# Merging two matmuls that share a stationary operand: u's high and low parts as one 512-column moving operand, with a PSUM pool of 6 + 2 banks

## The chip, the cores and the metric

The kernel runs on one core of one Trainium2 chip. The metric is the device time of one execution in microseconds (us). Three executions before the change took 1532.24, 1532.51 and 1533.59 us; their median, 1532.51 us, is the time that the prediction is made against. TensorE is called PE here, VectorE DVE, ScalarE ACT, GpSimd POOL; SP issues most DMAs.

## What is computed

One decoder layer on 256 tokens of width 2048, all in float32:

```python
u   = rmsnorm(h, norm_mix_pre)
z, xbc, dt_raw, q, k, v = split(u @ w_in)           # 2048 x 12320
y_ssm = SSD scan on silu(conv(xbc)), gate silu(z), grouped RMSNorm
y_att = dilated causal attention on q, k, v (16 heads of 128)
h   = h + rmsnorm(concat(y_ssm, y_att) @ w_out, norm_mix_post)
h   = h + rmsnorm(relu(rmsnorm(h) @ w_up)**2 @ w_down, norm_mlp_post)
```

The four weight matrices hold most of the work: w_in, w_out (4096 x 2048), w_up (2048 x 8192) and w_down (8192 x 2048). All are read once from HBM.

## The kernel before, in words

**Every product in three.** To keep float32 accuracy with PE's faster fp32r format, each operand is cut into a high part (rounded to fp32r) and a low part (what the rounding left). A product a·b becomes hi·hi + hi·lo + lo·hi, three matmuls into the same accumulator. `split` (line 117) makes the parts: ACT copies to the high part (line 120, or 123 with a scale), DVE subtracts it (line 121 or 124).

**Weights.** `weights` (line 126) loads a block of KB = 2 row tiles by 512 columns (512 KB) by a DMA on SP's queue into `raw` (4 buffers), and splits it into `hi` and `lo` (5 buffers each). All of it is issued under `tc.high_priority(offset=AHEAD)`. The order of instructions on each engine is not the order of the Python lines: a planner at build time places each engine's instructions by priority as soon as, by its own durations, their inputs and buffers are there. The finished order on each engine is fixed, and an instruction that waits holds up all behind it on its engine.

**Two kinds of product.** `gemm_tokens` (line 157) gives [token, feature] results: the activations are stationary, the weights move, 512 columns a matmul, three matmuls (lines 174, 175, 176) for each token half and row tile. It takes two accumulators of one PSUM bank each. It serves z, v, w_out, the first block of w_up and w_down. `gemm_features` (line 182) gives [feature, token] results: a 128x128 piece of the weights is stationary, and u moves, 256 tokens a matmul. For each row tile k (16) and each of four feature tiles f it issues line 197 (`hi`·`uh`), line 199 (`hi`·`ul`) and line 200 (`lo`·`uh`), into `acc[f // 2][:, f % 2]`, half a bank. It takes two accumulators of one bank each. There are 31 such calls: 8 for the convolved blocks (B, C, x), 8 for q and k, 15 for w_up. So each of the three lines runs 31 x 64 = 1984 times.

**PSUM.** Eight banks: pool `pacc` with 4 accumulators of one bank and pool `psm` with 4 of one bank, the latter handed out by `psmall` (line 108) to everything else: turned tiles of x (`turn_x`, 251), the SSD groups (`ssd_group`, 393), attention (486), `residual` (567).

**What reads the accumulators of gemm_features.** `conv_block` (368): DVE multiplies the accumulator by 1/rms into `pad` (line 375), then 16 DVE and 4 ACT instructions convolve. `queries` (515): DVE multiplies it into `cT` (line 519). The w_up loop (657): one DVE instruction does relu times 1/rms into `r` (line 660), then `hidden` squares it on ACT (616) and splits it. Each call has two such reads, b = 0 and 1, of 512 columns.

**Side work.** The SSD groups and attention heads are Python generators in the deque `waiting`; `pump` (146) runs one step after each weight block, so that their small matmuls stand between the blocks. Two SSD groups are under way at a time. A group's first step takes two `ps` buffers (lines 399, 410), its second one (433) that the third step still writes and reads (438 on PE, 440 on DVE), and the third step takes another (443) for the 16 matmuls of line 446.

**The start.** The first `gemm_features` call loads x as it goes: `turn_x` transposes a piece of x on PE (line 256) into a `ps` buffer and splits it into `uh` and `ul`. With `step=1` the weight block is loaded and split one row tile at a time.

## Time and profile before

| | |
|---|---|
| three executions | 1532.24, 1532.51, 1533.59 us |
| the profiled execution: its own time | 1533.54 us |
| its span, first to last instruction | 1531.8 us |
| matmuls recorded | 9701 |
| granted PE clock, mean | 0.999 |
| DVE busy, ACT busy, shares of the span | 57%, 47% |
| DMA: moved, mean rate | 283.38 MB, 185 GB/s |

How to read the views. The page lists each engine's busy time; a matmul's busy time includes its way through the array, and the next starts while it is still on that way, so the sum of busy times is more than the time PE needed. What one matmul costs in a dense row is the distance from its start to the start of the next, which the timeline shows. In the timeline the columns are start, duration, engine, line, operation, tiles (out<-in), shape and count. A row of a group gives count, busy time, mean duration in ns, and the idle time before it. A row of the waits gives who waited for whom: total us, times, longest.

### The profile page before, as it was taken

The numbers are of one execution on the slowest core, as the hardware profiler recorded it, in microseconds if no ns is written. First come the engines' busy times: TensorE is split into PE (matmuls) and PEld (weight loads), VectorE is DVE, ScalarE is ACT, GpSimd is POOL, SyncE is SP. The second block draws the span as 40 slices with busy tenths as digits, with TensorE's granted clock in tenths as the row PEclk, the third lists the DMA queues.
The fourth block names the chain that finished last, engine by engine and source line by source line (L and its number), as shares of the span: only waits on it lengthen the run. The fifth ranks groups of instructions, "written<-read, shape, count | busy, mean of one in ns | idle before, by whom it ended". The sixth has DMA issues, their size and how long they took to land.

```text
span 1531.8 us, 23944 instructions
## 1 busy us (share of the span) xinstructions
PE 1516.7 (99%) x9701; PEld 1384.2 (90%) x9701; DVE 874.8 (57%) x1196; ACT 713.3 (47%) x945; POOL 57.7 (4%) x73
## 2 busy tenths in 40 slices
PE   8999999999999999999999999999999999999997
PEld 8999999999999999888878999988889999988886
DVE  5777786875555454544457545544444555554444
ACT  6555564554535343544346444444444444444432
POOL 0002200220000000000000000000000000000000
PEclk9999999999999999999999999999999999999999
DMA  8565556555655555575556556555566666555553
GB/s 266 175 197 170 185 178 188 177 167 165 177 167 169 173 169 171 173 259 195 190 180 205 181 180 184 186 193 193 192 192 193 180 182 187 182 191 193 193 171 132
DMA packets 147951, 283.38 MB, mean 185 GB/s; under 512 B 11408, under 2 KB 14336, under 8 KB 147328
## 3 DMA queue, kind: packets, MB, share of 16 engines
q1 hardware_dynamic: 142576, 271.94, 57.1%
q10 hardware_dynamic: 5264, 9.91, 1.9%
q8 instruction: 76, 1.25, 0.3%
q14 instruction: 35, 0.29, 0.0%
HBM read 279.68 MB, written 2.13 MB: 184 GB/s over the span
## 4 chain that ended last, share of the span: by engine, by line
PE 98%; DMA 1%; DVE 1%; issue 0%; ACT 0%; POOL 0%; SPq 0%; POOLq 0%; DVEq 0%
PE acc L197 16%; PE acc L199 16%; PE acc L200 16%; PE acc L174 15%; PE acc L176 15%; PE acc L175 15%; PE ps L446 1%; PE ps L511 0%; PE ps L489 0%; DMA xs<-in_x_dram 0%; DMA raw<-in_w_in_dram 0%; PE ps L402 0%; PE ps L488 0%; PE ps L512 0%; PE ps L466 0%
## 5 line engine op out<-in xcount | busy, mean ns | idle before, releaser
L121 DVE TENSOR_TENSOR lo<-raw,hi 128x1024 fp32r<-128x1024 f32 (+1 forms) x520 | 629.4, 1212 | 575.6 <-ACT hi L120 574.3
L120 ACT ACTIVATE hi<-raw 128x1024 fp32r<-128x1024 f32 (+1 forms) x520 | 543.3, 1046 | 733.4 <-PE acc L176 332.7
L197 PE MATMUL acc<-uh,hi 128*128 128x256 f32 x1984 | 569.6, 288 | 1.8 <-ACT uh L123 1.8
L199 PE MATMUL acc<-ul,hi 128*128 128x256 f32 x1984 | 562.4, 284 | 0.0
L200 PE MATMUL acc<-uh,lo 128*128 128x256 f32 x1984 | 562.0, 283 | 0.0
L197 PEld LDWEIGHTS acc<-uh,hi 128*128 128x128 f32 x1984 | 380.9, 192 | 3.5 <-ACT uh L123 2.4
L199 PEld LDWEIGHTS acc<-ul,hi 128*128 128x128 f32 x1984 | 381.6, 192 | 1.3 <-DVE ul L124 0.4
L200 PEld LDWEIGHTS acc<-uh,lo 128*128 128x128 f32 x1984 | 381.4, 192 | 0.0
L174 PE MATMUL acc<-hi,sh 128*128 128x512 f32 x384 | 150.6, 392 | 0.0
L174 PE MATMUL acc<-hi,ah 128*128 128x512 f32 x384 | 149.9, 390 | 0.0
L175 PE MATMUL acc<-lo,sh 128*128 128x512 f32 x384 | 149.5, 389 | 0.0
L176 PE MATMUL acc<-hi,sl 128*128 128x512 f32 x384 | 149.4, 389 | 0.0
L176 PE MATMUL acc<-hi,al 128*128 128x512 f32 x384 | 149.4, 389 | 0.0
L175 PE MATMUL acc<-lo,ah 128*128 128x512 f32 x384 | 149.4, 389 | 0.0
L174 PE MATMUL acc<-hi,uh 128*128 128x512 f32 x288 | 112.5, 392 | 0.0
L176 PE MATMUL acc<-hi,ul 128*128 128x512 f32 x288 | 112.1, 391 | 0.0
L175 PE MATMUL acc<-lo,uh 128*128 128x512 f32 x288 | 112.0, 390 | 0.0
L176 PEld LDWEIGHTS acc<-hi,sl 128*128 128x128 f32 x384 | 72.1, 188 | 15.1
L176 PEld LDWEIGHTS acc<-hi,al 128*128 128x128 f32 x384 | 72.1, 188 | 15.0
L175 PEld LDWEIGHTS acc<-lo,ah 128*128 128x128 f32 x384 | 72.1, 188 | 14.9
L175 PEld LDWEIGHTS acc<-lo,sh 128*128 128x128 f32 x384 | 72.1, 188 | 14.8
L174 PEld LDWEIGHTS acc<-hi,sh 128*128 128x128 f32 x384 | 72.1, 188 | 14.8
(181 smaller groups left out, 962.2 us busy)
## 6 DMA issues: line engine op xcount, KB each, us to landing
raw<-in_w_in_dram SPq DMA_DIRECT2D x184, 512.0 KB, 3.6
raw<-in_w_up_dram SPq DMA_DIRECT2D x128, 512.0 KB, 3.6
raw<-in_w_down_dram SPq DMA_DIRECT2D x128, 512.0 KB, 3.6
raw<-in_w_out_dram SPq DMA_DIRECT2D x64, 512.0 KB, 4.1
raw<-in_w_in_dram SPq DMA_DIRECT2D x16, 256.0 KB, 5.2
bc<-acs_d ACTq DMA_DIRECT2D x8, 512.0 KB, 4.4
xs<-in_x_dram SPq DMA_DIRECT2D x8, 256.0 KB, 5.3
h<-in_x_dram ACTq DMA_DIRECT2D x1, 2048.0 KB, 12.0
```

The source lines that it names most:

```text
L120: nc.scalar.activation(hi, src, AF.Copy)
L121: nc.vector.tensor_tensor(lo, src, hi.bitcast(F32), op=ALU.subtract)
L174: nc.tensor.matmul(acc[t], a_h[:, r, ts], hi[:, j], start=k == 0, stop=False)
L175: nc.tensor.matmul(acc[t], a_h[:, r, ts], lo[:, j], start=False, stop=False)
L176: nc.tensor.matmul(acc[t], a_l[:, r, ts], hi[:, j], start=False, stop=k == nk - 1)
L197: nc.tensor.matmul(dst, hi[:, j, fs], uh[:, k], start=k == 0 and f % 2 == 0, stop=False, skip_group_check=True)
L199: nc.tensor.matmul(dst, hi[:, j, fs], ul[:, k], start=False, stop=False, skip_group_check=True)
L200: nc.tensor.matmul(dst, lo[:, j, fs], uh[:, k], start=False, stop=last, skip_group_check=True)
L446: nc.tensor.matmul(p[:, c, r], bc[:, r, c * P:(c + 1) * P], xdt[:, c, r], start=True, stop=True)
```

## The change

Five edits:

1. `uh` and `ul` become the two halves of one tile `u2` [128, 16, 2, 256], so that for one row tile the two parts lie side by side: 512 columns.
2. `gemm_features` multiplies `hi` by all 512 columns in one matmul, into a full bank whose first half collects hi·uh and whose second half collects hi·ul. The matmul `lo`·`uh` goes to the first half. Each accumulator is now a tile of two banks, two of them a call. The loops change places: feature tiles outside, the block's two row tiles inside.
3. `added` puts the halves together: ACT copies the second halves (512 columns) out of PSUM, DVE adds the first halves. It stands under `tc.high_priority(offset=AHEAD)`. The three readers then work on its result in SBUF: one ACT and one DVE instruction more for each of the 62 reads.
4. `pacc` has 3 tiles of two banks (6 banks), `psm` 2 of one bank. `gemm_tokens` takes one two-bank tile, a bank for each token half.
5. At the start one of the two-bank tiles, `spare`, stands in for the lost `ps` buffers: `turn_x` uses `psmall` and the banks of `spare` by turns.

```diff
-    pacc = ctx.enter_context(tc.tile_pool(name="pacc", bufs=4, space=bass.MemoryType.PSUM))
-    psm = ctx.enter_context(tc.tile_pool(name="psm", bufs=4, space=bass.MemoryType.PSUM))
+    pacc = ctx.enter_context(tc.tile_pool(name="pacc", bufs=3, space=bass.MemoryType.PSUM))
+    psm = ctx.enter_context(tc.tile_pool(name="psm", bufs=2, space=bass.MemoryType.PSUM))
...
-    uh = big.tile([P, NK, S], F32R, name="uh")
-    ul = big.tile([P, NK, S], F32R, name="ul")
+    u2 = big.tile([P, NK, 2, S], F32R, name="u2")
+    uh, ul = u2[:, :, 0], u2[:, :, 1]
...
-        acc = [pacc.tile([P, NB], F32, name="acc") for _ in range(NT)]
+        both = pacc.tile([P, NT, NB], F32, name="acc")
+        acc = [both[:, t] for t in range(NT)]
...
-        acc = [pacc.tile([P, 2, S], F32, name="acc") for _ in range(2)]
+        acc = [pacc.tile([P, 2, 2, S], F32, name="acc") for _ in range(2)]
...
-            for j in range(KB):
-                k = k0 + j
-                for f in range(4):
-                    dst = acc[f // 2][:, f % 2]
-                    fs = slice(f * P, (f + 1) * P)
-                    last = k == NK - 1
-                    nc.tensor.matmul(dst, hi[:, j, fs], uh[:, k], start=k == 0 and f % 2 == 0, stop=False,
+            for f in range(4):
+                fs = slice(f * P, (f + 1) * P)
+                bank = acc[f // 2][:, f % 2]
+                for j in range(KB):
+                    k = k0 + j
+                    nc.tensor.matmul(bank, hi[:, j, fs], u2[:, k], start=k == 0, stop=False, skip_group_check=True)
+                    nc.tensor.matmul(bank[:, 0], lo[:, j, fs], uh[:, k], start=False, stop=k == NK - 1,
                                      skip_group_check=True)
-                    nc.tensor.matmul(dst, hi[:, j, fs], ul[:, k], start=False, stop=False, skip_group_check=True)
-                    nc.tensor.matmul(dst, lo[:, j, fs], uh[:, k], start=False, stop=last, skip_group_check=True)
...
+    def added(dst, acc, tmp=None):
+
+        tmp = dst if tmp is None else tmp
+        with tc.high_priority(offset=AHEAD):
+            nc.scalar.activation(tmp, acc[:, :, 1], AF.Copy)
+            nc.vector.tensor_tensor(dst, acc[:, :, 0], tmp, op=ALU.add)
...
+    spare = pacc.tile([P, 2, NB], F32, name="acc")
+
     def turn_x(k0):
-        q = psmall().rearrange("p (f s) -> p f s", f=2)
+        i = k0 // KB
+        q = (spare[:, i // 2 % 2] if i % 2 else psmall()).rearrange("p (f s) -> p f s", f=2)
...
-            nc.vector.tensor_tensor(pad[:, :, 3:], acc[b], rbc[:, None, :].to_broadcast([P, 2, S]), op=ALU.mult)
+            added(pad[:, :, 3:], acc[b], dst[:, 2 * b:2 * b + 2])
+            nc.vector.tensor_tensor(pad[:, :, 3:], pad[:, :, 3:], rbc[:, None, :].to_broadcast([P, 2, S]), op=ALU.mult)
...
-            nc.vector.tensor_tensor(dst[:, 2 * b:2 * b + 2], acc[b], scale[:, None, :].to_broadcast([P, 2, S]),
-                                    op=ALU.mult)
+            d = dst[:, 2 * b:2 * b + 2]
+            added(d, acc[b])
+            nc.vector.tensor_tensor(d, d, scale[:, None, :].to_broadcast([P, 2, S]), op=ALU.mult)
...
-                nc.vector.scalar_tensor_tensor(r, acc[b], 0.0, rbc[:, None, :].to_broadcast([P, 2, S]),
+                added(r, acc[b])
+                nc.vector.scalar_tensor_tensor(r, r, 0.0, rbc[:, None, :].to_broadcast([P, 2, S]),
                                                op0=ALU.max, op1=ALU.mult)
```

## The prediction

> **What bounds the kernel now.** I read the page first: busy times, then the chain of work that ended last.
>
> ```profile
> span 1531.8 us, 23944 instructions
> ...
> PE 1516.7 (99%) x9701; PEld 1384.2 (90%) x9701; DVE 874.8 (57%) x1196; ACT 713.3 (47%) x945; POOL 57.7 (4%) x73
> ...
> PE 98%; DMA 1%; DVE 1%; issue 0%; ACT 0%; POOL 0%; SPq 0%; POOLq 0%; DVEq 0%
> PE acc L197 16%; PE acc L199 16%; PE acc L200 16%; PE acc L174 15%; PE acc L176 15%; PE acc L175 15%; PE ps L446 1%; PE ps L511 0%; PE ps L489 0%; DMA xs<-in_x_dram 0%; DMA raw<-in_w_in_dram 0%; PE ps L402 0%; PE ps L488 0%; PE ps L512 0%; PE ps L466 0%
> ```
>
> 98% of the chain is PE's, and half of that is the three lines of `gemm_features`. A busy PE could still hide waits, so the next view is PE's own waits between 40 and 1517 us:
>
> ```profile
> PE ps L580 <- PE acc L176: 0.5, 1, 0.5
> PE ps L580 <- DVE h L575: 0.4, 1, 0.4
> ```
>
> Two waits, 0.9 us in all. PE is dense, so the time is the number of matmuls times their distance from start to start. That distance comes from PE's timeline at the edges of two stretches of the MLP:
>
> ```profile
> 990.32 0.40 PE L174 MATMUL acc<-hi,sh 128*128 128x512 f32 x1
> ...
> 1164.20 0.39 PE L176 MATMUL acc<-hi,al 128*128 128x512 f32 x1
> 1164.42 0.28 PE L197 MATMUL acc<-uh,hi 128*128 128x256 f32 x1
> ...
> 1348.62 0.28 PE L200 MATMUL acc<-uh,lo 128*128 128x256 f32 x1
> 1348.74 0.40 PE L174 MATMUL acc<-hi,sh 128*128 128x512 f32 x1
> ```
>
> From 990.32 to 1164.42 lie four `gemm_tokens` calls of 32 row tiles: 4 x 32 x 2 x 3 = 768 matmuls of 512 columns in 174.10 us, **226.7 ns each**. From 1164.42 to 1348.74 lie eight `gemm_features` calls: 8 x 64 x 3 = 1536 matmuls of 256 columns in 184.32 us, **120.0 ns each**. Two of 256 cost 240.0, one of 512 costs 226.7: 13.3 ns go with the instruction and not with its columns.
>
> **The merge.** The line that goes and the one that grows run 1984 times each:
>
> ```profile
> L197 PE MATMUL acc<-uh,hi 128*128 128x256 f32 x1984 | 569.6, 288 | 1.8 <-ACT uh L123 1.8
> L199 PE MATMUL acc<-ul,hi 128*128 128x256 f32 x1984 | 562.4, 284 | 0.0
> ```
>
> Per step the three matmuls took 360.0 ns; after, one of 512 and one of 256 take 226.7 + 120.0 = 346.7. Saved: 13.3 ns x 1984 = **26.4 us**. This needs the two widths to alternate at the price that each has in a row of its own kind. The edge above shows one pair of each: 0.22 us from the 512-column matmul at 1164.20 to the 256-column one behind it, 0.12 us from the 256 at 1348.62 to the 512 behind it. The other worry is the loading of weights, of which one per step goes too: if a load were longer than the matmul that hides it, the 256-column one would be the bound. The floor for it shows at 16 matmuls of 64 columns:
>
> ```profile
> 132.76 1.73 PE ps L446 x16
> ```
>
> 1.73 / 16 = 108 ns, under 120: a load hides behind a 256-column matmul, as it does now. I take 26.4 us.
>
> The Trainium skill speaks against this size: "TensorE: Matmul & The Clock Gate", section "Back-to-back issue gap", has a warm matmul cost N/2.4 + 2.5 ns. By it 256 columns cost 109.2 and 512 cost 215.8, the merge saves 2.5 ns a step, an estimate of 5 us in all. Both distances measured here are above that rule, and their difference, the only thing that counts, is 13.3.
>
> **What is added, on ACT and DVE.** Each of the 62 reads gets an ACT copy and a DVE add of 512 columns out of PSUM. Nothing in the trace reads every second 256 columns; the nearest rows read a whole bank, and I take them:
>
> ```profile
> L670 ACT ACTIVATE mw<-acc 128x512 f32<-128x512 f32 x8 | 4.7, 589 | 1.2 <-PE acc L176 1.2
> L660 DVE SCALAR_TENSOR_TENSOR r<-acc,rbc 128x512 f32<-128x512 f32 x30 | 20.8, 692 | 0.4
> ```
>
> 62 x 0.589 = 36.5 us on ACT, 62 x 0.69 = 42.8 us on DVE, spread over the kernel, beside PE: cost nothing as long as nobody waits. DVE's load by stretch, from the windows (length, then busy PE, PEld, DVE, ACT, POOL, clock, DMA share, GB/s):
>
> ```profile
> 118.00:165.00 47.00, 47.00 (x318) 43.35 (x317) 39.56 (x78) 26.52 (x39) 10.82 (x12) 1.00 0.54 169
> 990.32:1164.42 174.10, 174.10 (x770) 144.15 (x769) 80.61 (x68) 73.73 (x75) 0.00 (x0) 1.00 0.60 193
> 1164.43:1348.73 184.30, 184.30 (x1537) 184.30 (x1536) 97.40 (x93) 82.04 (x93) 0.00 (x0) 1.00 0.62 184
> ```
>
> In the w_up stretch DVE goes from 53% to (97.4 + 16 x 0.69) / 177.5 = 61%. The tightest is the SSD stretch: 39.56 of 47 us, and with one call's two adds 41 of 46: 89%. Neither engine becomes the bound. Nor does the memory: the weights of the w_up stretch, 184 GB/s now, come to 184 x 184.3 / 177.5 = 191 GB/s, which the token stretch (193) shows to be had.
>
> **Where PE may have to wait: the hand-over of accumulators.** Three two-bank tiles in turn and two for each `gemm_features` call mean that where two such calls follow each other, the second tile of the later one is the first tile of the earlier. Counting the turns through the kernel gives 21 such hand-overs: 4 at the convolved blocks, 4 at k after q, 13 in w_up. The changed loop order works for it: the first tile (feature tiles 0 and 1) is done half a block before the call's end T, and wanted half a block after. A block is 8 steps x 347 ns = 2.77 us, so the tile is done at T - 1.39 and wanted at T + 1.39. In between must go the copy and the add. What else the two engines do then, around the call's end at 1187.46 in the stretch before:
>
> ```profile
> 1184.66 1.06 ACT L120 ACTIVATE hi<-raw 128x1024 fp32r<-128x1024 f32 x1 [1.82 <-PE acc L199]
> 1185.75 1.23 DVE L121 TENSOR_TENSOR lo<-raw,hi 128x1024 fp32r<-128x1024 f32 x1 [1.65 <-ACT hi L120]
> 1186.94 1.41 DVE L660 SCALAR_TENSOR_TENSOR r<-acc,rbc 128x512 f32<-128x512 f32 x2
> ```
>
> Each block's end releases a weight split: ACT 0.08 us after the end, then DVE at 1.2, done at 2.4. So with the shorter block ACT is free at T - 1.6, the copy runs from T - 1.3 to T - 0.7; DVE's split ends at T - 0.4, the add ends near T + 0.3. Wanted at T + 1.39: 1.1 us to spare. Behind the waiting copy on ACT stands the next weight split, behind the add the same on DVE; five weight buffers, some 11 us ahead, cover that. I take 0 for the hand-overs.
>
> **psm with two buffers.** In attention the steps come 3.5 us apart, and each takes one buffer:
>
> ```profile
> 399.21 0.43 PE ps L489 x2
> 402.74 0.43 PE ps L489 x2
> ```
>
> ```profile
> L489 PE MATMUL ps<-cT x32: 379/380/382, 399.0 to 632.2; 128*128 128x256 f32 x32
> L495 DVE CUSTOM_DVE_ANT_0 sm<-ps,cst x32: 291/355/423, 399.7 to 635.9; 128x128 f32<-128x128 f32 x16, 128x256 f32<-128x256 f32 x16
> ```
>
> With two, a buffer is wanted again after 7 us; the last one, written by 632.6, was read by 636.3, 3.7 us: 0. The SSD groups are tighter. With four buffers, the tile of line 446 was free at once; with two it is the tile that line 438 has just written, and must wait until DVE's line 440 has read it:
>
> ```profile
> 132.16 0.60 PE L438 MATMUL ps<-st,cT 128*128 128x256 f32 x2
> 132.59 0.55 PE L446 MATMUL ps<-xdt,bc 128*128 128x64 f32 x4
> ...
> 137.25 0.60 PE L438 MATMUL ps<-st,cT 128*128 128x256 f32 x2
> 137.68 0.44 PE L446 MATMUL ps<-xdt,bc 128*128 128x64 f32 x3
> ```
>
> ```profile
> 132.79 0.42 DVE L440 TENSOR_TENSOR yo<-ps,eacs 128x256 f32<-128x256 f32 x1 [1.54 <-PE ps L438]
> ...
> 139.10 0.42 DVE L440 TENSOR_TENSOR yo<-ps,eacs 128x256 f32<-128x256 f32 x1
> ```
>
> If PE stood still, it would lose 133.21 - 132.59 = 0.6 us for one group of a pair and 139.52 - 137.68 = 1.8 for the other, 4 x 2.4 = 9.8 us for eight groups. The planner may instead put matmuls of the running call in between, and then it is 0. I take **2 us**, nearer to 0, because such matmuls are always there. With them the moved groups cost PE nothing.
>
> **The start.** Here PE waits for x, and the memory is the bound (first row, 0.95 and 311 GB/s); its matmuls of 256 columns stand 0.21 us apart up to 15.5 us and 0.12 from then on:
>
> ```profile
> 5.00:15.00 10.00, 7.49 (x32) 6.79 (x33) 4.69 (x9) 5.61 (x13) 0.00 (x0) 1.00 0.95 311
> ```
>
> ```profile
> 15.04 0.41 PE L199 MATMUL acc<-ul,hi 128*128 128x256 f32 x1
> 15.25 0.41 PE L200 MATMUL acc<-uh,lo 128*128 128x256 f32 x1
> ...
> 15.94 0.28 PE L197 MATMUL acc<-uh,hi 128*128 128x256 f32 x1
> 16.06 0.28 PE L199 MATMUL acc<-ul,hi 128*128 128x256 f32 x1
> ...
> 32.03 1.04 PE L256 MATMUL ps<-cst,xs 128*128 128x128 f32 x8
> ```
>
> ```profile
> PE acc L197 <- ACT uh L123: 1.8, 2, 1.2
> PE ps L256 <- DMA xs<-in_x_dram: 2.4, 2, 1.3
> ```
>
> With the feature tiles outside, PE wants both row tiles of a block early, so the waits that there are (4.2 us) may come to twice that: +4. If the slow distance ends 20 matmuls sooner, that is 20 x 0.09 = 2 us: -2. I take **+1 us**. The second call, whose first tile is now `spare`, loses nothing that counts: the last pieces of x are transposed at 32.03, so the first call was still running then.
>
> **Sum.** -26.4 + 0 + 2 + 1 = -23.4 us. The profiled execution took 1533.54 us (span 1531.8 and 1.7 around it), 1.0 over the median of the three; against the median: 1532.5 - 23.4 = **1509 us**.
>
> **Rivals.**
>
> *A. As above*, 1503 to 1514: the merge, with 0 to 10 us of waits. Chance 0.62.
>
> *B. The merge pays, the waits take a good part.* The SSD stretch is where DVE is at 89%, and there both the hand-overs (4) and the two `ps` buffers (every step of eight groups) wait for DVE in its order. For it speaks that a read of `ps` already comes up to 2 us after PE's write (139.10 against 137.25); against it that PE waits nowhere now. Price: 9.8 us of the bound above and some half a us at each of 16 further steps: 1532.5 - 26.4 + 18 = 1524 at its end, 1514 at its near end. Chance 0.20.
>
> *C. The merge does not pay.* If a 512-column matmul over the two halves costs what two do, or only little less, the time is 1532.5 less a few: 1527 to 1535. Against it stand the 768 matmuls at 226.7. Chance 0.06: 0.02 for a gain of 5 us, 1527.5, and 0.04 for none. The figure of 2.5 ns in the Trainium skill's "TensorE: Matmul & The Clock Gate", "Back-to-back issue gap", would be the former.
>
> *D. Slower: the hand-over.* The place is the add of `added` on DVE at the 21 hand-overs. If the planner puts copy and add behind the weight split that the call's last block releases, ACT splits until T + 1.14, DVE until T + 2.37, and the add ends at T + 3.06, 1.67 us after PE wants the tile: 21 x 1.67 = 35 us, and 1532.5 - 26.4 + 35 = **1541 us**. It decides from 26.4 / 21 = 1.26 us a hand-over on. For it: the order is fixed at build time by the planner's durations, and splits and adds have the same offset. Against it: the add belongs to the earlier call and its input is there half a block sooner. Chance 0.12.
>
> **How the numbers follow.** A measurement of this kernel can tell about 0.2%, 3 us, from no change. Faster by more: A, B and the 0.02 of C, 0.84; within: the 0.04; slower: D, 0.12. The range takes all of A and nearly all of B: 1503 to 1525, about 0.8.
>
> **What the changed profile would show.** PE with 9701 - 1984 = 7717 matmuls; the w_up stretch of eight calls in 177.5 us instead of 184.32; the merged line 1984 times with 128x512, 0.227 us to the next start, and 0.12 after each `lo` matmul: that is step one, and C is dead or alive by it. Each `added` read: ACT near 0.59, DVE near 0.69 us; PE's waits without a row "acc <- DVE" above a us: the hand-over; 21 rows of 1 to 2 us would be D. In the SSD stretch matmuls of the running call between lines 438 and 446, or else a wait for DVE there: B. The prediction is wrong if PE's idle time between 40 and 1500 us comes to over 20 us, or if the start ends more than 4 us later.

## The result, and the profile after

The changed kernel took **1535.22 us** (median of 20 executions, 1533.75 to 1536.92), the kernel before 1532.74 in the same series (median of 20, 1530.66 to 1536.26): ratio 1.0014, 95% interval 1.0007 to 1.0021. That is 2.5 us more where 23.4 less were forecast. The profiled execution took 1536.6 us. The page of after, engines and chain:

```profile
span 1534.8 us, 20069 instructions
...
PE 1508.1 (98%) x7717; PEld 1279.6 (83%) x7717; DVE 914.2 (60%) x1258; ACT 751.8 (49%) x1007; POOL 56.7 (4%) x73
...
PE 96%; DVE 1%; ACT 1%; DMA 1%; issue 1%; SPq 0%; POOLq 0%; POOL 0%; DVEq 0%; ACTq 0%
PE acc L198 30%; PE acc L177 15%; PE acc L175 15%; PE acc L199 15%; PE acc L176 15%; PE ps L457 1%; DVE lo L121 1%; ACT hi L120 1%; PE ps L500 0%; PE ps L522 0%; DMA xs<-in_x_dram 0%; ACT junk L600 0%; DVE u L124 0%; DMA raw<-in_w_in_dram 0%; PE ps L413 0%
```

The 1984 matmuls are gone: 7717 are left. Still the chain is 96% PE's, so the time has to be in their distances and in PE's waits. In after, line 198 is the merged matmul, 199 the one with `lo`, 208 and 209 are `added`, 175 to 177 are `gemm_tokens`. Cutting both timelines at the changes between feature and token products shows where it went (us; the start is counted from the first feature matmul, at 7.29 before and 7.32 after):

| stretch | calls of `gemm_features` | before | after | difference | merge at 6.7 ns a pair | rest |
|---|---|---|---|---|---|---|
| start, to the first token matmul | 3 | 85.9 | 93.3 | +7.4 | -1.3 | +8.7 |
| SSD groups and gates | 7 | 302.8 | 299.3 | -3.5 | -3.0 | -0.5 |
| q, k, v and attention | 6 | 201.1 | 198.7 | -2.5 | -2.6 | +0.1 |
| w_out, first half of w_up | 7 | 393.3 | 396.7 | +3.5 | -3.0 | +6.5 |
| w_down, first half | 0 | 174.1 | 174.1 | 0 | 0 | 0 |
| w_up, second half | 8 | 184.3 | 180.9 | -3.4 | -3.4 | 0 |
| the rest, to the end of the span | 0 | 183.0 | 184.4 | +1.4 | 0 | +1.4 |

The 6.7 ns come from the stretch that has nothing but merged products. PE's timeline of after at its two ends and in its middle:

```profile
1169.42 0.39 PE L198 MATMUL acc<-u,hi 128*128 128x512 f32 x1
...
1181.08 0.40 PE L198 MATMUL acc<-u,hi 128*128 128x512 f32 x1
1181.31 0.28 PE L199 MATMUL acc<-u,lo 128*128 128x256 f32 x1
1181.42 0.40 PE L198 MATMUL acc<-u,hi 128*128 128x512 f32 x1
...
1182.13 0.40 PE L198 MATMUL acc<-u,hi 128*128 128x512 f32 x1
...
1350.31 0.40 PE L175 MATMUL acc<-hi,sh 128*128 128x512 f32 x1
```

From 1169.42 to 1350.31 lie 8 x 64 = 512 pairs in 180.89 us: **353.3 ns a pair**, where 346.7 were forecast and the three matmuls cost 360.0 before: 6.7 saved. Three pairs, 1181.08 to 1182.13, take some 1.06 us again and again; on the mean a wide matmul is followed after 236.5 ns, a narrow one after 116.8. That PE waits for nothing there, its waits for the whole kernel show (who waited for whom: total us, times, longest):

```profile
PE acc L198 <- DVE u L124: 6.0, 5, 2.0
PE ps L266 <- DMA xs<-in_x_dram: 3.4, 2, 3.0
PE acc L177 <- DVE u L124: 2.1, 2, 1.6
PE acc L175 <- ACT u L123: 2.0, 4, 0.8
PE acc L175 <- DVE mw L577: 1.7, 1, 1.7
PE ps L232 <- DVE half L221: 1.1, 1, 1.1
PE acc L175 <- DVE mw L655: 0.8, 1, 0.8
PE ps L592 <- DVE u L124: 0.3, 2, 0.2
PE ps L592 <- issue: 0.2, 1, 0.2
```

No row has PE waiting for `r`, `cT` or `pad`, the results of line 209: the hand-over of accumulators costs nothing. The waits belong to two places, the start (lines 198, 266 and 232) and the residual behind w_out and at the end (175, 177, 592). The groups of `added` on DVE and ACT cost what was forecast:

```profile
L209 DVE TENSOR_TENSOR r<-acc,r 128x512 f32<-128x512 f32 x30 | 20.5, 684 | 0.0
L208 ACT ACTIVATE r<-acc 128x512 f32<-128x512 f32 x30 | 17.7, 589 | 7.1 <-PE acc L199 7.1
```

So there were three questions: why is the pair dear, what costs the start 8.7 us, and what costs the residual 6.5 and the end 1.4?

### The profile page after: what moved, and what is told of

Same layout as the page of the kernel before. It is cut to its first block, busy times and chain, and to the rows that moved or that the text cites. A ratio compares the mean times of both kernels' runs of the same rounds, so it can differ in the third digit from the quotient of the medians.

```text
span 1534.8 us, 20069 instructions
## 1 busy us (share of the span) xinstructions
PE 1508.1 (98%) x7717; PEld 1279.6 (83%) x7717; DVE 914.2 (60%) x1258; ACT 751.8 (49%) x1007; POOL 56.7 (4%) x73
## 4 chain that ended last, share of the span: by engine, by line
PE 96%; DVE 1%; ACT 1%; DMA 1%; issue 1%; SPq 0%; POOLq 0%; POOL 0%; DVEq 0%; ACTq 0%
PE acc L198 30%; PE acc L177 15%; PE acc L175 15%; PE acc L199 15%; PE acc L176 15%; PE ps L457 1%; DVE lo L121 1%; ACT hi L120 1%; PE ps L500 0%; PE ps L522 0%; DMA xs<-in_x_dram 0%; ACT junk L600 0%; DVE u L124 0%; DMA raw<-in_w_in_dram 0%; PE ps L413 0%
## 5 line engine op out<-in xcount | busy, mean ns | idle before, releaser
L198 PE MATMUL acc<-u,hi 128*128 128x512 f32 x1984 | 717.9, 405 | 6.1 <-DVE u L124 6.0
L199 PE MATMUL acc<-u,lo 128*128 128x256 f32 x1984 | 559.6, 282 | 0.0
L198 PEld LDWEIGHTS acc<-u,hi 128*128 128x128 f32 x1984 | 375.6, 189 | 97.4 <-DVE u L124 8.0
L199 PEld LDWEIGHTS acc<-u,lo 128*128 128x128 f32 x1984 | 377.6, 190 | 1.1
L175 PE MATMUL acc<-hi,u 128*128 128x512 f32 x288 | 113.2, 393 | 2.0 <-ACT u L123 2.0
L177 PE MATMUL acc<-hi,u 128*128 128x512 f32 x288 | 112.9, 392 | 2.1 <-DVE u L124 2.1
L176 PE MATMUL acc<-lo,u 128*128 128x512 f32 x288 | 112.2, 390 | 0.0
L175 PEld LDWEIGHTS acc<-hi,ah 128*128 128x128 f32 x384 | 72.1, 188 | 18.1 <-DVE mw L577 2.1
L177 PEld LDWEIGHTS acc<-hi,u 128*128 128x128 f32 x288 | 54.1, 188 | 14.5 <-DVE u L124 3.1
```

The lines of the kernel that those rows point to most:

```text
L175: nc.tensor.matmul(acc[t], a_h[:, r, ts], hi[:, j], start=k == 0, stop=False)
L176: nc.tensor.matmul(acc[t], a_h[:, r, ts], lo[:, j], start=False, stop=False)
L177: nc.tensor.matmul(acc[t], a_l[:, r, ts], hi[:, j], start=False, stop=k == nk - 1)
L198: nc.tensor.matmul(bank, hi[:, j, fs], u2[:, k], start=k == 0, stop=False, skip_group_check=True)
L199: nc.tensor.matmul(bank[:, 0], lo[:, j, fs], uh[:, k], start=False, stop=k == NK - 1, skip_group_check=True)
```

## The experiments

The kernel before, run beside them, had medians of 1532.81 us (the first four), 1532.69 (the next four), 1532.03 (the three behind these) and 1532.85 (the last). Shares of the whole are read from medians, stretches from single profiles; the start moves by 2 or 3 us from one profile to another, so for it the medians decide.

### The price of a pair

The first theory was that each change between wide and narrow costs; the rival, that two matmuls in succession into the same bank do.

**e1**: of the changed kernel, the two `hi` matmuls of a feature tile first, then the two `lo`. Half as many changes of width.

```diff
                     nc.tensor.matmul(bank, hi[:, j, fs], u2[:, k], start=k == 0, stop=False, skip_group_check=True)
+                for j in range(KB):
+                    k = k0 + j
                     nc.tensor.matmul(bank[:, 0], lo[:, j, fs], uh[:, k], start=False, stop=k == NK - 1,
```

> The changed kernel with the order of the four matmuls of a feature tile and block changed from hi, lo, hi, lo to hi, hi, lo, lo. In the changed kernel a hi/lo pair takes 353.3 ns in the long stretches and 346.7 in a few short ones, with the forecast's prices (226.7 and 120.0) only in the latter. Theory A (the alternation of widths costs it: each change of width may cost some ns): half as many changes of width, so a pair between 346.7 and 350, the eight w_up calls in 177.5 to 179.2 us instead of 180.9, the whole kernel 6 to 13 us below the changed one. Rival B (the pair costs what it costs because two matmuls of a pair write one bank and the second adds where the first has just written): no change, 353 ns, same time. Rival C (a weight load before a 512-column matmul is late): the pair changes by under 2 ns.

Measured: 1527.80 us (6 executions), ratio 0.9967 (0.9954 to 0.9979). PE's timeline at the ends of the w_up stretch:

```profile
1164.69 0.39 PE L198 MATMUL acc<-u,hi 128*128 128x512 f32 x1
...
1343.03 0.40 PE L175 MATMUL acc<-hi,sh 128*128 128x512 f32 x1
```

178.34 us / 512 = 348.3 ns a pair, 5.0 less than after, from the order alone. For the whole kernel that is 9.9 us by the rows (5.0 x 1984) and 7.4 by the medians (1535.22 less 1527.80). But the extra isn't where a change of width is: a wide matmul is followed after 232.9 ns by a wide one and after 233.3 by a narrow one, a narrow one after 114.6 by a narrow and 115.8 by a wide.

**e7** goes further, all eight `hi` of a block and then all eight `lo`; **e8** keeps after's alternation but puts the row tiles outside, so that each pair goes to another bank than the one before it.

```diff
@@ e7 @@
                     nc.tensor.matmul(bank, hi[:, j, fs], u2[:, k], start=k == 0, stop=False, skip_group_check=True)
+            for f in range(4):
+                fs = slice(f * P, (f + 1) * P)
+                bank = acc[f // 2][:, f % 2]
+                for j in range(KB):
+                    k = k0 + j
                     nc.tensor.matmul(bank[:, 0], lo[:, j, fs], uh[:, k], start=False, stop=k == NK - 1,
@@ e8 @@
-            for f in range(4):
-                ...
-                for j in range(KB):
+            for j in range(KB):
+                k = k0 + j
+                for f in range(4):
```

> The changed kernel with a block's eight hi matmuls first and its eight lo matmuls behind, so that the width changes twice a block and not sixteen times. Theory A (each change of width costs): away from the hand-overs a pair takes 346.7 to 347.5 ns, against 353.3 for hi, lo, hi, lo and 348.4 for hi, hi, lo, lo. Rival B (the price comes from writing one bank twice running): also low here, as the bank changes after two matmuls, so the next run tells these two apart. The first tile is done later in this order, so waits for DVE at the 21 hand-overs of up to a us each are expected, and the whole is no faster than with hi, hi, lo, lo.

> The changed kernel with the loops as before: row tiles outside, feature tiles inside, hi and lo alternating, so that each pair goes to another bank than the one before. Theory A (change of width): 353 ns a pair as in the changed kernel. Rival B (the same bank four matmuls running): below 350. The first tile is now done only 0.7 us before a call's end and wanted 0.7 us after it, so PE should wait for DVE's add at the 21 hand-overs: the add is expected near 0.9 us after the end, some 0.3 us each.

Measured, one execution each: e7 1532.37 us, its w_up stretch 1167.24 to 1346.12, 349.4 ns a pair; e8 1533.82 us, 1167.17 to 1347.48, 352.2 ns on the mean. With a quarter of e1's changes of width e7 is no cheaper than e1: the extra doesn't go with the number of changes, and the first theory falls. (e7's PE waits for `pad`, 3.2 us in all, lie before this stretch.) Another bank for each pair doesn't take the extra away: six of the eight calls of e8's stretch run at 353.3, as after does; the other two are dealt with below. And in e10 below four matmuls in succession into one bank cost no more than others. So the rival falls too. e8 shows something else in PE's waits:

```profile
PE acc L198 <- DVE cT L209: 0.8, 1, 0.8
PE acc L198 <- DVE pad L209: 0.8, 1, 0.8
```

These are the hand-overs of accumulators, which after doesn't have. The changed order of the loops does buy that, for 1.6 us.

**e9** leaves the narrow matmul out, **e10** makes it 512 wide (`lo` times both halves). No widths mix in either.

```diff
@@ e9 @@
-                    nc.tensor.matmul(bank, hi[:, j, fs], u2[:, k], start=k == 0, stop=False, skip_group_check=True)
-                    nc.tensor.matmul(bank[:, 0], lo[:, j, fs], uh[:, k], start=False, stop=k == NK - 1,
+                    nc.tensor.matmul(bank, hi[:, j, fs], u2[:, k], start=k == 0, stop=k == NK - 1,
                                      skip_group_check=True)
@@ e10 @@
-                    nc.tensor.matmul(bank[:, 0], lo[:, j, fs], uh[:, k], start=False, stop=k == NK - 1,
+                    nc.tensor.matmul(bank, lo[:, j, fs], u2[:, k], start=False, stop=k == NK - 1,
                                      skip_group_check=True)
```

> The changed kernel without the matmuls lo times uh of the feature products (its result leaves these terms out): 1984 matmuls of 512 columns, nothing of another width between them. So far a wide matmul took 236.5 ns between narrow ones and 231 in runs of eight, against 226.7 in the token products. If the mixture of widths makes the price (theory A in what is left of it), they stand 226.7 ns apart here, 14.5 us a w_up call; if it is something of these operands (weights stationary, both parts of u moving, a change of bank after two matmuls), 231 ns or more.

> The changed kernel with lo, too, times both parts of u, into both halves of the bank (adds the term lo times ul): as many matmuls as in the changed kernel, all 512 columns wide. By the mixture of widths: 226.7 ns each, a pair 453.4, 29.0 us a w_up call. By the operands or the bank changing after four matmuls: 229 to 233 each.

Measured: e9 1310.02 us; where no wait stands between them its merged matmuls are 226.9 ns apart (61 distances from 1096.33 to 1110.17). e10 1732.9 us; its w_up stretch on PE's timeline:

```profile
1314.35 0.39 PE L198 MATMUL acc<-u,hi 128*128 128x512 f32 x1
...
1546.45 0.39 PE L175 MATMUL acc<-hi,sh 128*128 128x512 f32 x1
```

232.10 us / 1024 = 226.7 ns each. The merged operand, two halves in one bank, costs exactly what any 512 columns cost. The forecast's price for the wide matmul was right, and so was the 120.0 for the narrow one in a row of its kind. It is the **mixture** that costs 1.6 (e1) to 6.6 ns (after) a pair more than their sum, in most stretches.

The physical reason stays open. What it has to explain is that the same pairs, in the same order, also run at the forecast's price in some stretches. Here after's PE timeline near 203 us:

```profile
203.20 0.28 PE L199 MATMUL acc<-u,lo 128*128 128x256 f32 x1
203.32 0.39 PE L198 MATMUL acc<-u,hi 128*128 128x512 f32 x1
203.55 0.28 PE L199 MATMUL acc<-u,lo 128*128 128x256 f32 x1
```

0.35 us from narrow to narrow, for some 13 us (199.5 to 212.3), and then 353 again, with the same instructions at the same granted clock. In e8 two whole calls of the w_up stretch do so. PE's timeline in one of them, and in a later call:

```profile
1192.60 0.39 PE L198 MATMUL acc<-u,hi 128*128 128x512 f32 x1
...
1211.67 0.39 PE L198 MATMUL acc<-u,hi 128*128 128x512 f32 x1
...
1237.16 0.40 PE L198 MATMUL acc<-u,hi 128*128 128x512 f32 x1
...
1257.30 0.40 PE L198 MATMUL acc<-u,hi 128*128 128x512 f32 x1
```

The first two rows are 55 pairs apart: 19.07 us, 346.7 ns each. The last two are 57 apart: 20.14 us, 353.3 each. So the 352.2 of e8 is a mean of two prices, and the choice of banks doesn't decide between them. In after the price changes where small matmuls of the side work stand in between; in e8 it also changes where one call meets the next, with no side work there. The weight loads show no difference: in both of these calls each is recorded right behind the start of the matmul before it and lasts 0.19 us. In e1 no second price shows: its stretches without side work run at 348.2 to 348.5.

### The start

Three things had changed there: which banks `turn_x` uses, the order of the loops, and the merging, which makes PE wait for u's low part before the first product of a row tile. **e3** and **e4** put the two `psm` buffers alone into the kernel before, e3 with two spare banks of their own for the start, e4 with two of the four accumulators as `spare`.

```diff
@@ e3 @@
-    psm = ctx.enter_context(tc.tile_pool(name="psm", bufs=4, space=bass.MemoryType.PSUM))
+    psm = ctx.enter_context(tc.tile_pool(name="psm", bufs=2, space=bass.MemoryType.PSUM))
+    spx = ctx.enter_context(tc.tile_pool(name="spx", bufs=2, space=bass.MemoryType.PSUM))
...
-        q = psmall().rearrange("p (f s) -> p f s", f=2)
+        q = (spx.tile([P, NB], F32, name="sx") if k0 // KB % 2 else psmall()).rearrange("p (f s) -> p f s", f=2)
@@ e4 @@
-    psm = ctx.enter_context(tc.tile_pool(name="psm", bufs=4, space=bass.MemoryType.PSUM))
+    psm = ctx.enter_context(tc.tile_pool(name="psm", bufs=2, space=bass.MemoryType.PSUM))
...
+    spare = [pacc.tile([P, 2, S], F32, name="acc") for _ in range(2)]
...
-        q = psmall().rearrange("p (f s) -> p f s", f=2)
+        i = k0 // KB
+        q = spare[i // 2 % 2] if i % 2 else psmall().rearrange("p (f s) -> p f s", f=2)
```

> The kernel before, with two ps buffers instead of four, and two banks of their own that stand in at the start as spare does (4 + 2 + 2 banks). No merge. Theory: two ps buffers cost the changed kernel its time behind the second residual (transposes wait for a buffer, some 4 us of the 6.2 us lost between 795 and 840) and little in the SSD stretch: 3 to 5 us slower than before, start unchanged. Rival: two buffers cost nothing there and the loss at 800 is all from the tiles of two banks or from u in one tile: within 1 us of before.

> The kernel before, with two ps buffers, and the start's spare banks taken out of the four accumulators as in the change (4 + 2 banks), so that the second feature product can't begin while x is turned. No merge, loops as before. Theory: the changed kernel lost 8 to 9 us up to 100 us because PE has nothing else to do while the last pieces of x are split, so that it waits and its granted clock drops to a half (35 to 39 and 45 to 49 us): this kernel is 6 to 9 us slower in that stretch than before, and shows dropped clocks after 30 us. Rival: the start is lost by the loops' new order (row tiles inside feature tiles): here it is within 2 us of before.

Measured: e3 1536.13 us (10), 1.0024 (1.0015 to 1.0034); e4 1537.23 (5), 1.0032 (1.0019 to 1.0045). Their starts take 83.7 and 85.1 us, not more than the 85.9 of before: the bank plan is not what delays the start. Both are slower all the same, by what the next part tells.

**e5** takes the merging out of the first product and gives it its old order, with one two-bank tile as its accumulators; **e6** keeps it merged and gives it the old order alone (row tiles outside).

```diff
@@ e5, in gemm_features @@
+            if first:
                 for j in range(KB):
                     k = k0 + j
-                    nc.tensor.matmul(bank, hi[:, j, fs], u2[:, k], start=k == 0, stop=False, skip_group_check=True)
-                    nc.tensor.matmul(bank[:, 0], lo[:, j, fs], uh[:, k], start=False, stop=k == NK - 1,
+                    for f in range(4):
+                        dst = acc[f // 2][:, f % 2]
+                        ...
+                        nc.tensor.matmul(dst, hi[:, j, fs], uh[:, k], start=k == 0 and f % 2 == 0, stop=False,
+                        nc.tensor.matmul(dst, hi[:, j, fs], ul[:, k], start=False, stop=False,
+                        nc.tensor.matmul(dst, lo[:, j, fs], uh[:, k], start=False, stop=last,
@@ e6, in gemm_features @@
+            if first:
                 for j in range(KB):
                     k = k0 + j
+                    for f in range(4):
+                        ...
+                        nc.tensor.matmul(bank, hi[:, j, fs], u2[:, k], start=k == 0, stop=False, skip_group_check=True)
+                        nc.tensor.matmul(bank[:, 0], lo[:, j, fs], uh[:, k], start=False, stop=k == NK - 1,
```

> The changed kernel, but the first feature product (the one that loads x) stays as before: three matmuls of 256 columns, row tiles outside, result in the two banks of one tile, read without adding. So one accumulator tile more is free at the start. The start up to the first token product took 85.9 us before and 93.3 in the changed kernel (90.4 and 90.6 in two of its variants). Theory M (the merged matmul and the loops' order make PE wait for the low part of u, 6 us in five waits, and for both row tiles): the start is back at 85 to 87 us, 5 to 7 below the changed kernel. Rival P (the bank plan at the start): 89 us or more. The kernel before with that bank plan alone lost about 1 us there, which speaks for M.

> The changed kernel, with row tiles outside and feature tiles inside in the first feature product alone, still merged. If the loops' order is what costs the start, the first token product begins 85 to 88 us after the first feature matmul; if it is the merge itself (the first matmul of a row tile needs u's low part, which DVE makes after ACT has made the high part), it stays at 90 to 93 us with PE's waits for DVE on u at 4 us or more.

Measured: e5 1529.53 us (10), 0.998 (0.997 to 0.999); e6 1531.12 (10), 0.9993 (0.9981 to 1.0005). Against after's 1535.22 the old order alone gives back 4.1 us, and taking the merging out as well 1.6 more (2.0, since e5 gives up 64 x 6.7 ns = 0.4 of it): together **6.1 us**. What the merging costs there shows in e6's PE waits:

```profile
PE acc L199 <- DVE u L124: 4.7, 3, 2.0
```

Before, u's low part (`ul`, written last) was wanted by the second matmul of a step, and PE had the first to do meanwhile. In after, this wait and the order come together, and a wait can have a second price. The windows of after in the start (length, busy PE, PEld, DVE, ACT, POOL, granted clock, DMA share, GB/s):

```profile
33.00:39.00 6.00, 5.13 (x19) 4.19 (x20) 2.35 (x7) 1.29 (x3) 0.00 (x0) 0.72 0.70 237
39.00:45.00 6.00, 3.96 (x26) 3.44 (x26) 3.43 (x6) 2.65 (x5) 0.14 (x2) 1.00 0.52 120
45.00:50.00 5.00, 4.95 (x20) 4.00 (x19) 2.51 (x4) 1.88 (x3) 0.00 (x0) 0.66 0.45 120
```

The same windows of e5:

```profile
33.00:39.00 6.00, 5.91 (x45) 5.38 (x44) 3.38 (x5) 2.70 (x5) 0.14 (x2) 1.00 0.74 201
39.00:45.00 6.00, 6.00 (x44) 5.58 (x43) 4.34 (x6) 3.18 (x4) 0.00 (x0) 1.00 0.38 101
45.00:50.00 5.00, 5.00 (x39) 4.74 (x38) 5.00 (x10) 3.07 (x4) 0.00 (x0) 1.00 0.90 268
```

A granted clock of 0.72 over 6 us, with half as the only lower value in the record, is 3.4 us at half speed, and 0.66 over 5 us the same. The second of them follows this wait on PE's timeline of after:

```profile
41.80 0.61 PE L291 MATMUL ps<-dg,ones 128*128 128x128 f32 x4
44.45 0.50 PE L198 MATMUL acc<-u,hi 128*128 128x512 f32 x1 [2.04 <-DVE u L124]
```

So some 2 us of idle PE were followed by 3.4 us at half clock, up to 1.7 us more. It isn't always so: in e8 a wait of the same length, up to 40.8 us, was followed by 9 us at a clock of 1.00. And it differs between runs of one order: e2 below has after's PE order in the start and takes 90.4 us for it instead of 93.3. It has one such stretch there where after has two, and its slow distances of the first microseconds end at 15.7 us, after's at 18.1.

The gain from undoing both is clear of noise: the longest execution of e5 (1531.85 us) is shorter than the shortest of after (1533.75). How the 6.1 us divide between the order and the merging is not clear, since the intervals of e5 and e6 overlap.

### The residual

In the w_out stretch the suspects were the two `psm` buffers (e3, e4) and the tile of two banks that both token halves share. **e2** gives the token products whose second half runs behind the first (the last block of w_out, the first of w_up, the last of w_down) two tiles, one for each half.

```diff
-        both = pacc.tile([P, NT, NB], F32, name="acc")
-        acc = [both[:, t] for t in range(NT)]
+        if lag:
+            acc = [pacc.tile([P, NT, NB], F32, name="acc")[:, 0] for _ in range(NT)]
+        else:
+            both = pacc.tile([P, NT, NB], F32, name="acc")
+            acc = [both[:, t] for t in range(NT)]
```

> The changed kernel, but the three token products with a lag take two accumulator tiles, one bank used in each, instead of the two banks of one tile. Theory: in the changed kernel PE waits for the reading of the first token half's bank before it writes the second half's bank of the same tile (1.65 us at 800.5, 0.8 at 1519); with two tiles both waits go, and the kernel ends 2.5 to 3 us earlier. Rival: the waits are for the arithmetic behind (the residual's chain is late anyway), and a wait of the same length appears a few matmuls later: under 1 us gained at 800, 0.9 at the end.

Measured: 1529.94 us (10), ratio 0.998 (0.9971 to 0.999): **5.3 us** under after. In its profile the stretch to the end of the residual takes 236.2 us instead of 238.6, and the last one 183.4 instead of 184.4: 3.4 us. The other 2 us are not placed by these two profiles, but the clock is a likely place. Every other changed kernel that keeps the two `mw` waits (e1, e5 to e10) has one or two stretches of 3.4 us at half clock in the residual, e5's from 799.1 to 802.5 us for instance; in the profiles of after and e2 none fell there. Over all executions the granted clock was 0.9957 on the mean in after (20) and 0.9971 in e2 (10); as an estimate, the difference over 1535 us is worth 2.1 us. What went away can be seen in after's timeline of all engines (in brackets the idle time and its releaser):

```profile
798.47 0.39 PE L177 MATMUL acc<-hi,al 128*128 128x512 f32 x1
...
798.90 0.60 ACT L576 ACTIVATE junk<-acc 128x512 bf16<-128x512 f32 x1 [0.30 <-PE acc L177]
...
799.77 0.68 DVE L577 TENSOR_TENSOR mw<-acc,wpost 128x512 f32<-128x512 f32 x1
...
800.51 0.50 PE L175 MATMUL acc<-hi,ah 128*128 128x512 f32 x1 [1.65 <-DVE mw L577]
```

One token half is finished at 798.47 and read by ACT and DVE; PE has the other half to do, in the other bank of the same tile, and starts only when the reading is over. In the kernel before, at the same point, it went on during the read:

```profile
798.30 0.68 DVE L565 TENSOR_TENSOR mw<-acc,wpost 128x512 f32<-128x512 f32 x1
798.36 0.39 PE L176 MATMUL acc<-hi,al 128*128 128x512 f32 x1
...
798.59 0.39 PE L174 MATMUL acc<-hi,ah 128*128 128x512 f32 x1
```

In e2's waits the rows with `mw` are gone, and PE's wait for u behind them, two rows of 4.1 us in after, comes to 1.1:

```profile
PE acc L180 <- DVE u L124: 0.7, 1, 0.7
...
PE acc L178 <- ACT u L123: 0.4, 1, 0.4
```

The two buffers are the other part: with them alone, the w_out stretch takes 397.7 us in e3 and 397.1 in e4, against 393.3 before, **+4.4 and +3.8**; by the medians it is +3.3 for the whole kernel in e3 and +4.4 in e4. e3's profile has 3.4 us at half clock in that stretch (803.7 to 807.2), e4's none, so e4's 3.8 is the cleaner figure. How two buffers cost that is shown in part only: PE's waits there grow from 0.9 us before to 2.1 in e4. The SSD groups, where the forecast looked for the cost, lose 0.8 us in e3 and in e4.

### All of it together

**e11** puts the answers into one kernel: `hi`, `hi`, `lo`, `lo`; the first product not merged; six accumulators of one bank each, so that nothing shares a tile, with `added` on one bank at a time; and the residual's turned tiles alternately from both pools. **e12** is e11 with each merged matmul cut in two again, so that only the merge differs.

```diff
@@ e11 against after @@
-    pacc = ctx.enter_context(tc.tile_pool(name="pacc", bufs=3, space=bass.MemoryType.PSUM))
+    pacc = ctx.enter_context(tc.tile_pool(name="pacc", bufs=6, space=bass.MemoryType.PSUM))
...
-        both = pacc.tile([P, NT, NB], F32, name="acc")
-        acc = [both[:, t] for t in range(NT)]
+        acc = [pacc.tile([P, NB], F32, name="acc") for _ in range(NT)]
...
-        acc = [pacc.tile([P, 2, 2, S], F32, name="acc") for _ in range(2)]
+        acc = [pacc.tile([P, 2, S], F32, name="acc") for _ in range(2 if first else 4)]
...
-            nc.scalar.activation(tmp, acc[:, :, 1], AF.Copy)
-            nc.vector.tensor_tensor(dst, acc[:, :, 0], tmp, op=ALU.add)
+            for f in range(2):
+                nc.scalar.activation(tmp[:, f], acc[f][:, 1], AF.Copy)
+                nc.vector.tensor_tensor(dst[:, f], acc[f][:, 0], tmp[:, f], op=ALU.add)
...
-                p = psmall()
+                p = pacc.tile([P, NB], F32, name="acc") if n % 2 else psmall()
@@ e12 against e11 @@
-                        nc.tensor.matmul(bank, hi[:, j, fs], u2[:, k], start=k == 0, stop=False, skip_group_check=True)
+                        nc.tensor.matmul(bank[:, 0], hi[:, j, fs], uh[:, k], start=k == 0, stop=False,
+                                         skip_group_check=True)
+                        nc.tensor.matmul(bank[:, 1], hi[:, j, fs], ul[:, k], start=False, stop=False,
+                                         skip_group_check=True)
```

> What the runs so far point to, together: merged matmuls in the order hi, hi, lo, lo (348.4 ns a pair), the first feature product as before the change, six accumulators of one bank each instead of three of two (a feature product takes four, added by quarters; a token product two, so that reading one half doesn't hold up the writing of the other), and residual using accumulators and ps buffers by turns. Sum against the kernel before: 30 calls x 64 x 11.6 ns = -22 us, residual stretch 0 to +2, SSD stretch +1, start -2 to +1: 1510 to 1514 us. If the finer adding makes the hand-overs late (4 ACT and 4 DVE instructions instead of 2 and 2 a call), waits for DVE on accumulators appear and it ends at 1516 to 1522.

> The six-accumulator kernel (1514.5 us) with each merged matmul taken apart again into two of 256 columns, hi times uh into the first half of the bank and hi times ul into the second; everything else stays, the adding of the halves too. So this is the merge by itself. If the prices per pair are all there is (348.4 ns with, 360.0 without), 30 calls x 64 x 11.6 = 22.3 us slower: 1536 to 1538 us, the stretch of eight w_up calls 184.3 us. If the kernel's other changes (accumulators, first product) made the gain, it is under 1525.

Measured: e11 **1514.51 us** (4 executions, 1512.78 to 1515.4), ratio 0.9889 (0.9872 to 0.9905), faster than both kernels. e12 1534.56 (7), 1.0023 (1.001 to 1.0036). The merge by itself is worth 20.0 us between the two. The w_up stretch of e11 on PE's timeline:

```profile
1149.38 0.39 PE L211 MATMUL acc<-u,hi 128*128 128x512 f32 x1
...
1327.71 0.40 PE L174 MATMUL acc<-hi,sh 128*128 128x512 f32 x1
```

and that of e12:

```profile
1164.56 0.28 PE L211 MATMUL acc<-u,hi 128*128 128x256 f32 x1
...
1348.88 0.40 PE L174 MATMUL acc<-hi,sh 128*128 128x512 f32 x1
```

178.33 us are 348.3 ns a pair, 184.32 are 360.0 for three: 11.7 x 30 x 64 = 22.5 us by the rows, 20.0 by the medians. Against the kernel before, e12 shows what all the rest costs when nothing is merged: 1.7 us. Its w_out stretch, with two `ps` buffers but with the residual's turned tiles taken from both pools, takes 394.2 us, 0.9 more than before where e4 took 3.8 more. PE's waits in e11, of which the main rows follow, have neither `mw` nor a wait for u's low part at the start:

```profile
PE ps L350 <- DVE both L346: 1.7, 1, 1.7
...
PE acc L199 <- ACT u L123: 0.7, 1, 0.7
PE acc L176 <- DVE u L124: 0.7, 1, 0.7
```

## Why the prediction was wrong

Its sum, term by term (medians where there are some):

| term | forecast | measured | from |
|---|---|---|---|
| the merge | -26.4 | -13.3 | 31 x 64 x 6.7 ns |
| hand-over of accumulators | 0 | 0 | after's waits |
| `psm` with two buffers | +2 | +3.3 | e3 (e4: +4.4) |
| the start | +1 | +6.1 | after less e5 |
| token halves in one tile | none | +5.3 | after less e2 |
| sum | -23.4 | +1.4 | after: +2.5 |

The measured terms come from different kernels, so they need not add up to the whole; that their sum comes so near is in part luck.

1. **The merge: the size was off by half.** The prediction said that the sum "needs the two widths to alternate at the price that each has in a row of its own kind", and took two single transitions at the edge of a stretch (0.22 and 0.12 us) as proof. One transition of each kind can't show a price of a steady mixture: stretches at 346.7 and at 353.3 have the same transitions (after, e8). Uniform rows keep the price (e10, 226.7; e12, 120.0); mixed ones mostly don't (348.3 to 353.3). The Trainium skill, "TensorE: Matmul & The Clock Gate", section "Back-to-back issue gap", has a fixed 2.5 ns beside the columns for a matmul by itself, which gave an estimate of 5 us for the merge. The measured 13.3 lies between that and my 26.4; with the order of e1, 11.7 ns a pair, it is far nearer to mine.

2. **The start: +1 with a bound of +4, and it came to +6.1.** The step took the waits of before and doubled them. It left out that the merged matmul needs both parts of u, so that PE loses the work it used to do while the low part was made, and that an idle stretch of 2 us can be followed by half clock. It also took 2 us off for slow distances that would end sooner: they ended at 15.2 us in e1, 15.7 in e2 and 18.1 in after, against 15.6 before. It did say that more than 4 us here would make it wrong. The one thing about the start that it argued at length, the bank that `spare` stands in for, costs nothing that e3 and e4 can show.

3. **`psm`: near in size, wrong about the place.** The SSD groups lose 0.8 us (e3, e4) against the 2 taken, so rival B (1514 to 1524, DVE in the SSD stretch) has no part in it. The residual, where u is turned through `ps` between w_out and w_up, was not looked at, though PE's only two waits of before past the start (line 580) stood in just that stretch.

4. **The token halves in one tile: not priced at all.** The change's list says so ("one two-bank tile, a bank for each token half"), and the prediction treated it as a matter of names. It makes one thing of two for whoever waits: PE's writes to one bank then stand behind ACT's and DVE's reads of the other, as the rows at 798 us show and e2, which gives each half a tile of its own, confirms.

5. **Right:** the hand-over (rival D, 1541, didn't happen; the first tile's add is done before it is wanted, and e8, without the changed order, shows 1.6 us); 0.589 us on ACT and 0.684 on DVE for each half of `added`; neither of them a bound at 49% and 60%; 7717 matmuls; the price of the merged matmul in a row of its kind (not the 0.227 and 0.12 us to the next start, which came to 0.2365 and 0.1168). Rival C gave nearly the measured time, but by chance: its mechanism, a 512-column matmul that costs as much as two, is refuted by e10. The 108 ns for matmuls of 64 columns, read from a group's length, are 111 to 112 by their starts, which changes nothing.

The forecast of 20 us or more of PE's idle time as the mark of failure was also too coarse: the waits of the whole kernel are 17.6 us, and the time was still lost, half of the 26 us by which the forecast missed through distances that no view of waits lists.

## What to carry to other kernels

Price a stream of matmuls by a stretch with the same mixture and order of widths, not by adding the prices of uniform rows; where there is none, try the orders, since `hi`, `hi`, `lo`, `lo` instead of `hi`, `lo` was worth 5 ns a pair here. When buffers are joined into one tile, list who reads one part while another is written, and when operands are joined into one instruction, list what the engine used to do while the second was still being made. A gain of 13 us (20 with e1's order) can be there and be spent again in three small places; undoing each alone finds them, and e11 keeps most of the gain: 17.5 us against the kernel before.

## What the runs showed of the hardware

- The same pairs of a 512- and a 256-column matmul, in the same order and at a granted clock of 1.0, ran at one of two prices, 346.7 or 353.3 ns, and kept it for many pairs on end: some 13 us at 346.7 in after, some 20 us at either price in e8. With two of each kind in a row they took 348.3, with eight 349.4. Why is open.
- A PE wait of 2.0 us inside otherwise dense work was followed by some 3.4 us at half clock in after and e2, and by none in e8. The Trainium skill, "TensorE: Matmul & The Clock Gate", section "HAM oscillation — how this bites in real kernels", gives as its abstract rule that idle gaps should not be over about 3.4 us. These traces show that less can be enough.
- In the slow first microseconds of after (granted clock 0.50 from 7.9 to 18.1 us) a 256-column matmul was followed after 0.21 us and a 512-column one after 0.43 (17.09, 17.30 and 17.73 us). There a 512-column matmul cost what two of 256 cost, and nothing of the 13.3 ns that the merge was to save shows.
- Reading every second 256 columns of two banks costs ACT 0.589 us and DVE 0.684, the same as a whole bank in a row (0.589 for ACT at line 670 before, 0.68 for DVE at line 577).
